# Two plain input-projection tiles of group A instead of four, and an eleventh pair computed with seven products

## The chip, the cores and the metric

The kernel runs on one core of one Trainium2 chip, as one program and one launch. The metric is the device time of an execution in microseconds (us), lower is better. An execution consists of the span, from the first to the last instruction of the program, and about 2 us around it.

## The reference

One step of a one-layer streaming encoder with two groups of attention heads, in float32. 640 tokens are processed together: 512 of a prompt and 8 x 16 of samples that extend cached sequences.

```python
def rmsnorm(x, g):
    return x * rsqrt(mean(x * x, -1) + 1e-6) * g

def layer(x):                                   # d_model 2048, x: 640 tokens
    p = rmsnorm(x, norm_mix) @ w_in             # columns: q, k, v of A (1024 each), q of B (1024), k, v of B (128 each)
    ...
    oa = band_attend(qa, ka, va, bias)          # 16 heads of 64: own chunk of 64 frames and 8 before, learned bias
    ob = band_attend(rope(qb), rope(kb), vb, sink)   # 16 query heads, 2 kv heads, window 128, sinks
    x = x + concat(rmsnorm(oa, g_a), rmsnorm(ob, g_b)) @ w_out
    h = rmsnorm(x, norm_ffn)
    x = x + (silu(h @ w_gate) * (h @ w_up)) @ w_down     # d_ff 5632
    return rmsnorm(x, norm_final)
```

Sample tokens attend to cached keys and values (256 of group A, 128 of group B) and to their own 16 frames. The new keys and values of both groups are returned too.

## The kernel before

Activations lie transposed, features on the 128 partitions and the 640 tokens along the free dimension, in two halves of 320. Every dense matmul is made of three (`mm3`, lines 207 to 209): both operands are split into a high and a low part (`split`: ScalarE makes the high part at L198, VectorE the low part at L199), and high x high, high x low and low x high are added up in PSUM. Each of these matmuls is 128 x 128 x 320.

The input projection gives 24 tiles of 128 features for group A, named (i, p): i is 0 for queries, 1 for keys, 2 for values, and p runs from 0 to 7. A tile is computed in one of two ways.

- **Plain** (`proj`, `dense`): 16 steps over the 2048 features, 2 token halves, 3 matmuls: 96 matmuls in a PSUM tile `dn`. Its evacuation is L382 or L384. After the six matmuls of a step `dense` calls `tick`, which lets side steps be written (`pump`), on average `n.rate` for each tick.
- **A pair by seven products** (`quartet`, `collect`): two output tiles, two token halves and two halves of the features form a 2 x 2 block product, which Strassen's scheme in Winograd's form makes with seven block products instead of eight: 7 x 8 x 3 = 168 matmuls for two tiles. The products read sums of activation blocks (`sums`). The first product's evacuation is L768, on ScalarE.

Sums of activation blocks are side work: `combine(k0, k1)` loads two tiles of x for each of its steps (L825, L826), scales one on ScalarE (L831), forms sums on VectorE (L832, L839) and GpSimd (L833, L835) and splits them. A third sum for each step is split later, in the first pair (`split_thirds`). Its x tiles use the two-tile slots of list W.

The other side work in this part is the rest of group B's attention: `prompt_b` for the prompt (queue "heads") and `decode_b` for the samples (queue "decode"). `decode_b` goes through eight batches, 0 to 7, with loads of cached keys (L552) and values (L553) ahead of batches 0 and 4. A batch is a chain of steps: scores of two kv heads on TensorE (L567, which the text calls the score), row maximum and sign on VectorE (L572, L573), exponents on ScalarE (L577, L578), normalization on VectorE (L579 to L582), four transposes on TensorE (L313), a copy on ScalarE (L592), the product with the values on TensorE (L597, called the weighing) and a copy on VectorE (L600). At its end `decode_b` stores its output (L603) and queues the last `combine(6, 8)`.

`pump` takes the streams in turn and writes one step of one of them. `drain` writes steps until none is left, `drain_queue` until one queue is empty, and `get` calls `pump` too while no slot of the wanted list is free. What is written is then ordered, engine by engine, by a scheduler that keeps dependences and puts ready work of other parts in between; `keep_pace` adds that a side matmul never stands before a plain or pair matmul that was written ahead of it. Engines and queues work through their instructions in the order so fixed.

After group B's eight query tiles the program reaches the loop at line 866: four plain tiles of group A, (1, 7), (0, 7), (2, 6) and (2, 7), at a rate of 1.15, with `drain_queue("heads")` after the second and `drain()` after the fourth. Ten pairs follow in the order of the list `order` (line 881); beside the last pair the heads of group A begin. Then come the output projection, the gate, up and down projections, and the final norm.

Of the kernel before, what the change touches and what calls it, by code (L numbers as in the profile page):

```python
# [291 lines left out]
def build(nc, tc, io, pools):  # L292
    n = Net(nc, tc, io, pools)
# [21 lines left out]
    def cut(hl, a, b):  # L315
        return hl[0][:, a:b], hl[1][:, a:b]
# [60 lines left out]
    def proj(idx, lst, ps=None, gain=None):  # L377
        if ps is None:
            ps = n.dense([(io["w_in"][idx, :, k:k + 8], 8) for k in (0, 8)], acts)
        out = n.get(lst)  # L380
        if gain is None:
            nc.vector.tensor_tensor(halves(out[:, :TOK]), ps, halves(r_mix), ALU.mult)  # L382
        else:
            nc.vector.scalar_tensor_tensor(halves(out[:, :TOK]), ps, gain, halves(r_mix), ALU.mult, ALU.mult)  # L384
        return out
# [424 lines left out]
    def keep_a(i, p, x):  # L810
        if i:
            dma(out=io["o_ka" if i == 1 else "o_va"][p], in_=x)
        dma(out=qkv_d[i, p], in_=x)
        n.put("S", x)
# [4 lines left out]
    def combine(k0, k1):  # L819

        tt, st = nc.gpsimd.tensor_tensor, nc.vector.scalar_tensor_tensor
        third = n.get("S" if k0 == 6 else "W")
        for kt in range(k0, k1):
            a, c = n.get("W"), n.get("W")
            dma(out=a[:, :TOK], in_=io["xT"][:, kt])  # L825
            dma(out=c[:, :TOK], in_=io["xT"][:, kt + 8])  # L826
            yield
            g = g_mix[:, kt + 8:kt + 9]
            a11, a21, a12, a22 = a[:, :HT], a[:, HT:TOK], c[:, :HT], c[:, HT:TOK]
            s1, s2 = a[:, TOK:TOK + HT], c[:, TOK:TOK + HT]  # L830
            nc.scalar.activation(a[:, :TOK], a[:, :TOK], AF.Identity, scale=g_mix[:, kt:kt + 1])  # L831
            st(s1, a22, g, a21, ALU.mult, ALU.add)  # L832
            tt(s2, s1, a11, ALU.subtract)  # L833
            s3 = third[:, HT * (kt % 3):HT * (kt % 3) + HT]
            tt(s3, a21, a11, ALU.subtract)  # L835
            thirds.append((third, s3))
            for which, x in ((3, s1), (1, s2), (6, a12)):
                if which == 6:
                    st(a12, a12, g, s2, ALU.mult, ALU.subtract)  # L839
                t = n.get("S")  # L840
                sums[kt][which] = t, pack(t, HT)
                n.split(x, *sums[kt][which][1])
            n.put("W", a, c)
            yield
# [17 lines left out]
    n.streams = (("heads 0", "heads"), ("decode 0", "decode"), ("combine", "combine"))  # L862
    n.add("combine", combine(0, 3))
    n.add("decode", decode_b())
    n.rate = 1.15
    for i, p in ((1, 7), (0, 7), (2, 6), (2, 7)):
        keep_a(i, p, proj(8 * i + p, "S", None, None if i else 0.125))
        if (i, p) == (0, 7):
            n.drain_queue("heads")
            n.move("Q", "S", 4)  # L870
            n.add("combine", combine(3, 6))
# [6 lines left out]
    for kt in range(8):  # L878
        for which, k, part in ((0, kt, 0), (2, kt, 1), (4, kt + 8, 0), (5, kt + 8, 1)):
            sums[kt][which] = None, cut(acts[k], HT * part, HT * part + HT)  # L880
    order = [(i, p + z) for p in range(0, 6, 2) for i in (1, 0, 2) for z in range(2)] + [(1, 6), (0, 6)]

    def group_operands(o_d, gain, ssq, tiles):
        own, out = [], []
# [509 lines left out]
```

## Time and profile before

| what | value |
|---|---|
| median of 3 runs | 2552.12 us (2551.49 to 2553.27) |
| profiled execution | 2550.54 us, span 2548.8 us |
| granted TensorE clock, mean | 0.993 |
| evacuation of plain tile (1, 7) | 212.0 us after the span's start |
| evacuation of plain tile (2, 7) | 282.4 us |
| first evacuations of pairs 1 and 10 | 286.75 and 516.13 us |

Times in the views are microseconds from the start of the span, unless a column says ns. PE is TensorE, PEld its weight loads, DVE VectorE, ACT ScalarE, POOL GpSimd, SP SyncE, which issues most of the DMAs. A row of the timeline gives start, duration, engine, line, operation, output<-inputs, shape and count, and in brackets the idle time before it and what ended that. Matmuls are pipelined: one takes 0.31 us from start to end, but they start 0.147 us apart in a full stream.

### The profile page before, as it was taken

The numbers are of one execution on the slowest core, as the hardware profiler recorded it, in microseconds if no ns is written. First come the engines' busy times: TensorE is split into PE (matmuls) and PEld (weight loads), VectorE is DVE, ScalarE is ACT, GpSimd is POOL, SyncE is SP. The second block draws the span as 40 slices with busy tenths as digits, with TensorE's granted clock in tenths as the row PEclk, the third lists the DMA queues.
The fourth block names the chain that finished last, engine by engine and source line by source line (L and its number), as shares of the span: only waits on it lengthen the run. The fifth ranks groups of instructions, "written<-read, shape, count | busy, mean of one in ns | idle before, by whom it ended". The sixth has DMA issues, their size and how long they took to land.

```text
span 2548.8 us, 44678 instructions
## 1 busy us (share of the span) xinstructions
PE 2496.6 (98%) x17325; PEld 2423.7 (95%) x17325; DVE 1949.0 (76%) x2928; ACT 1058.2 (42%) x1701; POOL 706.6 (28%) x568
## 2 busy tenths in 40 slices
PE   8999999999999999999999999999999999999997
PEld 8888899988789999999999999999999999999997
DVE  6666767685577787788888888888889877777797
ACT  5445333365455544344343334434334333333343
POOL 1001111120021123333232332323335433333353
PEclk9999999999999999999999999999999999999998
DMA  6234433376864434443334334434437756666655
GB/s 196 86 95 132 145 121 128 135 244 214 281 206 145 136 135 141 142 161 131 129 128 149 120 123 146 133 127 133 141 120 254 245 166 176 175 172 177 179 155 181
DMA packets 191605, 401.68 MB, mean 158 GB/s; under 512 B 22497, under 2 KB 83937, under 8 KB 191393
## 3 DMA queue, kind: packets, MB, share of 16 engines
q1 hardware_dynamic: 167056, 344.75, 41.5%
q0 software_dynamic: 23184, 52.77, 7.3%
q8 instruction: 136, 2.23, 0.4%
q10 hardware_dynamic: 1152, 1.31, 0.2%
q14 instruction: 77, 0.62, 0.1%
HBM read 311.14 MB, written 86.87 MB: 156 GB/s over the span
## 4 chain that ended last, share of the span: by engine, by line
PE 66%; DVE 4%; DMA 2%; issue 1%; ACT 1%; SPq 0%; DVEq 0%; ACTq 0%
PE dn L207 13%; PE dn L209 13%; PE dn L208 13%; PE at L209 9%; PE at L208 9%; PE at L207 9%; DVE W L199 2%; DVE S L759 1%; DMA W<-w_down 1%; PE at L313 0%; DVE S L1277 0%; DVE S L1085 0%; ACT S L410 0%; DVE W L737 0%; DMA x_d<-S 0%
## 5 line engine op out<-in xcount | busy, mean ns | idle before, releaser
L198 ACT ACTIVATE W<-W 128x1024 fp32r<-128x1024 f32 (+2 forms) x662 | 640.5, 968 | 1053.0 <-PE dn L208 558.8
L207 PE MATMUL dn<-S,W 128*128 128x320 f32 x3374 | 1058.3, 314 | 8.7 <-ACT W L198 5.7
L209 PE MATMUL dn<-S,W 128*128 128x320 f32 x3374 | 1047.2, 310 | 7.9 <-DVE W L199 7.9
L208 PE MATMUL dn<-S,W 128*128 128x320 f32 x3374 | 1045.4, 310 | 0.3 <-DVE S L199 0.3
L199 DVE TENSOR_TENSOR W<-W,W 128x1024 fp32r<-128x1024 f32 (+2 forms) x662 | 777.5, 1175 | 77.9 <-ACT W L198 74.3
L207 PEld LDWEIGHTS dn<-S,W 128*128 128x128 f32 x3374 | 635.5, 188 | 29.2 <-issue 17.2
L209 PEld LDWEIGHTS dn<-S,W 128*128 128x128 f32 x3374 | 634.9, 188 | 14.3 <-DVE W L199 11.8
L208 PEld LDWEIGHTS dn<-S,W 128*128 128x128 f32 x3374 | 635.6, 188 | 1.4 <-issue 0.9
L209 PE MATMUL at<-S,W 128*128 128x320 f32 x1834 | 568.8, 310 | 5.1 <-DVE W L199 5.0
L207 PE MATMUL at<-S,W 128*128 128x320 f32 x1834 | 568.3, 310 | 0.7 <-ACT W L198 0.7
L208 PE MATMUL at<-S,W 128*128 128x320 f32 x1834 | 567.8, 310 | 0.0
L740 POOL TENSOR_TENSOR W<-W,W 128x1024 f32<-128x1024 f32 (+2 forms) x85 | 183.2, 2156 | 754.7 <-DVE W L199 609.8
L209 PEld LDWEIGHTS at<-S,W 128*128 128x128 f32 x1834 | 345.3, 188 | 7.5 <-DVE W L199 7.5
L207 PEld LDWEIGHTS at<-S,W 128*128 128x128 f32 x1834 | 345.4, 188 | 1.1 <-ACT W L198 1.1
L208 PEld LDWEIGHTS at<-S,W 128*128 128x128 f32 x1834 | 345.5, 188 | 0.0
L759 DVE TENSOR_TENSOR S<-S,dn 128x320 f32<-128x320 f32 x398 | 182.2, 480 | 91.0 <-PE dn L209 90.4
L749 POOL TENSOR_TENSOR W<-W,W 128x1024 f32<-128x1024 f32 (+2 forms) x85 | 188.2, 2214 | 197.4 <-DVE W L199 145.4
L759 DVE TENSOR_TENSOR S<-S,at 128x320 f32<-128x320 f32 x292 | 137.7, 480 | 79.6 <-PE at L209 78.8
L735 DVE TENSOR_TENSOR W<-W,W 128x1024 f32<-128x1024 f32 (+2 forms) x86 | 135.0, 1570 | 70.0 <-DMA W<-w_down 35.8
L737 DVE TENSOR_TENSOR W<-W,W 128x1024 f32<-128x1024 f32 (+2 forms) x86 | 97.6, 1135 | 54.9 <-DMA W<-w_up 28.8
L1048 POOL DMA_DIRECT2D S<-act_d x161 | 88.0, 547 | 177.6 <-PE dn L209 92.1
L1112 DVE TENSOR_TENSOR S<-S,half 128x320 fp32r<-128x320 f32 x147 | 119.9, 836 | 1.9
(157 smaller groups left out, 1693.4 us busy)
## 6 DMA issues: line engine op xcount, KB each, us to landing
S<-act_d POOLq DMA_DIRECT2D x161, 320.0 KB, 3.8
W<-w_gate SPq DMA_DIRECT2D x88, 512.0 KB
W<-w_up SPq DMA_DIRECT2D x88, 512.0 KB
W<-w_in SPq DMA_DIRECT2D x66, 512.0 KB
W<-w_down SPq DMA_DIRECT2D x64, 384.0 KB
act_d<-half SPq DMA_DIRECT2D x147, 160.0 KB
act_d<-S SPq DMA_DIRECT2D x147, 160.0 KB
W<-w_down SPq DMA_DIRECT2D x68, 320.0 KB
```

Source lines behind the costliest of these rows:

```text
L198: self.nc.scalar.activation(hi, src, AF.Identity)
L199: self.nc.vector.tensor_tensor(lo, src, f(hi), ALU.subtract)
L207: mm(out, a[0], b[0], start=first, stop=False)
L208: mm(out, a[0], b[1], start=False, stop=False)
L209: mm(out, a[1], b[0], start=False, stop=last)
L735: nc.vector.tensor_tensor(b12[:, w], b12[:, w], b22[:, w], sub)
L737: nc.vector.tensor_tensor(s6[:, w], b11[:, w], b12[:, w], sub)
L740: eng.tensor_tensor(b11[:, w], b22[:, w], s6[:, w], sub)
L749: eng.tensor_tensor(b21[:, w], b21[:, w], s6[:, w], sub)
L759: add = lambda o, a, b: nc.vector.tensor_tensor(o, a, b, ALU.add)
L1048: nc.gpsimd.dma_start(out=r(sh(t, 2, HT)), in_=r(act_d[which, :, j]))
L1112: nc.vector.tensor_tensor(r(src), src, hi, ALU.subtract)
```

## The change

The loop of plain tiles keeps (1, 7) and (0, 7) alone, and the rate of side steps beside them is doubled from 1.15 to 2.3. `drain_queue("heads")`, the four slots and `combine(3, 6)` follow the first of the two tiles instead of the second of four. Tiles (2, 6) and (2, 7) become an eleventh pair at the end of the list, so that they are also the pair beside which group A's heads begin.

```diff
-    n.rate = 1.15
-    for i, p in ((1, 7), (0, 7), (2, 6), (2, 7)):
+    n.rate = 2.3
+    for i, p in ((1, 7), (0, 7)):
         keep_a(i, p, proj(8 * i + p, "S", None, None if i else 0.125))
-        if (i, p) == (0, 7):
+        if i:
             n.drain_queue("heads")
             n.move("Q", "S", 4)
             n.add("combine", combine(3, 6))
     n.drain()
...
-    order = [(i, p + z) for p in range(0, 6, 2) for i in (1, 0, 2) for z in range(2)] + [(1, 6), (0, 6)]
+    order = [(i, p + z) for p in range(0, 6, 2) for i in (1, 0, 2) for z in range(2)] + [(1, 6), (0, 6), (2, 6), (2, 7)]
```

How instructions move is seen in the order of each engine. First TensorE, around batch 5 of decode. Before, the weighing of batch 4 and the score of batch 5 are followed by the end of plain tile (2, 6), `dn_2667`, and the beginning of (2, 7), `dn_2930`:

```order
L597 MATMUL at_2878<-S_492_2870,S_470_2767 64x128 x2
L597 MATMUL at_2878<-S_492_2870,S_5_83 64x128 x2
L567 MATMUL at_2890<-S_469_2766,S_471_2768 128x144
L567 MATMUL at_2892<-S_469_2766,S_471_2768 128x144
L209 MATMUL dn_2667<-S_70_215,W_477_2786 128x320
L207 MATMUL dn_2667<-S_70_215,W_476_2785 128x320
L208 MATMUL dn_2667<-S_71_216,W_476_2785 128x320
L209 MATMUL dn_2667<-S_70_215,W_477_2786 128x320
L207 MATMUL dn_2930<-S_10_93,W_507_2932 128x320
```

Now, from the weighing of batch 3 on, TensorE's order is this:

```order
L597 MATMUL at_2610<-S_454_2598,S_346_2138 64x128 x2
L597 MATMUL at_2610<-S_454_2598,S_5_83 64x128 x2
L567 MATMUL at_2675<-S_461_2636,S_463_2638 128x144
L567 MATMUL at_2677<-S_461_2636,S_463_2638 128x144
L313 MATMUL at_2711<-cst,S_475_2684 128x128 x2
L313 MATMUL at_2711<-cst,S_479_2697 128x128 x2
L597 MATMUL at_2718<-S_481_2716,S_462_2637 64x128 x2
L597 MATMUL at_2718<-S_481_2716,S_5_83 64x128 x2
L567 MATMUL at_2730<-S_461_2636,S_463_2638 128x144
L567 MATMUL at_2732<-S_461_2636,S_463_2638 128x144
L313 MATMUL at_2772<-cst,S_488_2739 128x128 x2
L313 MATMUL at_2772<-cst,S_492_2752 128x128 x2
```

The matmuls of plain tiles no longer stand between the steps of batches 3 to 7: up to the weighing of batch 2 both orders have 192 of them, and behind it the new order has none before the transposes of batch 7, where the first pair begins.

Second ScalarE, at batch 3. `at_2634` and `at_2636` are the scores of its two kv heads before, L198 splits, L831 scales an x tile of `combine`, L592 is the copy after the transposes:

```order
L577 ACTIVATE S_445_2643,sm_2639<-at_2634,sm_2638 128x144
L578 ACTIVATE sm_2640<-sm_2638,gains 128x1
L198 ACTIVATE S_466_2750<-W_463_2730 128x320
L198 ACTIVATE S_467_2753<-W_464_2731 128x320
L577 ACTIVATE S_449_2656,sm_2652<-at_2636,sm_2651 128x144
L578 ACTIVATE sm_2653<-sm_2651,gains 128x1
L198 ACTIVATE S_468_2757<-W_464_2731 128x320
L592 ACTIVATE S_462_2722<-at_2717 128x512
L831 ACTIVATE W_473_2780<-W_473_2780,gains 128x640
```

Now, from the second kv head of batch 3 (`at_2523`) to the first of batch 4 (`at_2675`):

```order
L831 ACTIVATE W_465_2644<-W_465_2644,gains 128x640
L577 ACTIVATE S_441_2543,sm_2539<-at_2523,sm_2538 128x144
L578 ACTIVATE sm_2540<-sm_2538,gains 128x1
L198 ACTIVATE S_34_143<-W_447_2568 128x320
L592 ACTIVATE S_454_2598<-at_2593 128x512
L198 ACTIVATE S_467_2659<-W_465_2644 128x320
L198 ACTIVATE S_468_2662<-W_466_2645 128x320
L831 ACTIVATE W_526_2897<-W_526_2897,gains 128x640
L198 ACTIVATE S_469_2666<-W_466_2645 128x320
L577 ACTIVATE S_475_2684,sm_2680<-at_2675,sm_2679 128x144
```

The scaling of x tile 5 now stands ahead of batch 3's second exponent, and that of x tile 6 ahead of batch 4's first.

Third the queue of SP, where the loads of x (L825, L826), the cached keys and values of the second four batches (L552, L553), weights of pairs (L722) and the stores of tile (1, 7) (L812, L813) stand. Before:

```order
L812 DMA o_ka<-S_393_2382 128x640
L813 DMA qkv_d<-S_393_2382 128x640
L825 DMA W_463_2730<-xT 128x640
L213 DMA W_475_2784<-w_in 128x1024
L213 DMA W_506_2931<-w_in 128x1024
L826 DMA W_464_2731<-xT 128x640
L813 DMA qkv_d<-S_450_2664 128x640
L552 DMA S_469_2766<-ckb 128x4x128
```

Now:

```order
L722 DMA W_566_3204<-w_in 128x1024
L812 DMA o_ka<-S_442_2551 128x640
L813 DMA qkv_d<-S_442_2551 128x640
L826 DMA W_456_2607<-xT 128x640
L553 DMA S_462_2637<-cvb 128x512
L825 DMA W_465_2644<-xT 128x640
L519 DMA ob_d<-S_431_2510 128x512
L552 DMA S_461_2636<-ckb 128x4x128
L826 DMA W_466_2645<-xT 128x640
L825 DMA W_526_2897<-xT 128x640
```

The weights of the removed tiles (L213) are gone, a weight tile of the second pair stands ahead, and the keys of the second four batches stand between loads of x.

## The prediction

> **What bounds the kernel now.** I read the page first, then windows of busy time by stage, then the timeline of single operations. The page:
>
> ```profile
> span 2548.8 us, 44678 instructions
> PE 2496.6 (98%) x17325; PEld 2423.7 (95%) x17325; DVE 1949.0 (76%) x2928; ACT 1058.2 (42%) x1701; POOL 706.6 (28%) x568
> ...
> PE 66%; DVE 4%; DMA 2%; issue 1%; ACT 1%; SPq 0%; DVEq 0%; ACTq 0%
> ```
>
> TensorE is busy for 98% of the span and makes two thirds of the chain that ended last, so a product fewer should be time gained, but only where TensorE really is the bound. That is read from the stages (us of the stretch, busy time of each engine with its instructions, granted clock, DMA share, GB/s):
>
> ```profile
> core 0: us, PE busy (x) PEld busy (x) DVE busy (x) ACT busy (x) POOL busy (x), PEclk, DMA share, GB/s
> 212.00:236.50 24.50, 23.66 (x166) 20.05 (x165) 16.78 (x73) 15.39 (x49) 3.50 (x7) 1.00 0.26 88
> 236.50:281.68 45.18, 41.69 (x295) 35.91 (x294) 32.22 (x98) 23.50 (x62) 6.98 (x15) 0.96 0.47 154
> 281.68:317.30 35.62, 32.24 (x200) 30.42 (x198) 27.01 (x28) 11.19 (x14) 8.96 (x4) 0.95 0.46 154
> 392.32:490.93 98.61, 98.30 (x671) 98.00 (x670) 67.50 (x72) 31.01 (x34) 19.25 (x8) 1.00 0.37 130
> ```
>
> The last row is four steady pairs of seven products: 4 x 168 = 672 matmuls in 98.61 us, 146.7 ns each, no idle time. There TensorE is the bound. The second row is the stretch in which the plain tiles (2, 6) and (2, 7) stand now, with the decode of group B beside them: their 192 matmuls take 192 x 0.1467 = 28.2 us of its 45.2, and the other 17 us are side matmuls, waits and a lower clock. So what matters is what fills this stretch once the 192 are gone.
>
> **The products.** Two plain tiles go (192 matmuls, 28.2 us), one pair comes (168). Its price is read from the first evacuations of successive pairs on ScalarE:
>
> ```profile
> 286.75 0.42 ACT L768 ACTIVATE S<-dn 128x320 f32<-128x320 f32 x1
> 317.30 0.42 ACT L768 ACTIVATE S<-dn 128x320 f32<-128x320 f32 x1
> ...
> 392.32 0.42 ACT L768 ACTIVATE S<-dn 128x320 f32<-128x320 f32 x1
> ...
> 490.93 0.42 ACT L768 ACTIVATE S<-dn 128x320 f32<-128x320 f32 x1
> ```
>
> Four steady pairs: 98.61 / 4 = **24.65 us** for one more. The first pair takes 317.30 - 286.75 = 30.55, 5.9 over that. On a TensorE that is always full the change would be worth 24 x 0.1467 = 3.5 us of gain. The two removed weight tiles and evacuations (ScalarE and VectorE) lie beside matmuls, and the eleventh pair's preparation lies beside its own, as the steady pairs show; I cost both at nothing.
>
> **The side work.** 2.3 x 32 ticks are as many calls as 1.15 x 64, 73.6, so the same side work is written; what changes is what stands beside it on TensorE. Up to the weighing (L597) of decode batch 2 both programs have 192 plain matmuls and the same batches. From there to the first pair the old order has 192 more, spread through batches 3 to 7; the new one has none until the last batch's transposes are through. TensorE takes its instructions in that order, so the stretch becomes as long as the chain of five batches: score (L567), row maximum and exponent, transposes (L313), copy (L592), weighing (L597), next score. Scores and weighings of the old run:
>
> ```profile
> 231.70 0.39 PE L567 MATMUL at<-S,S 64*128 64x144 f32 x2
> 236.52 0.44 PE L597 MATMUL at<-S,S 128*64 128x128 f32 x4
> 238.62 0.39 PE L567 MATMUL at<-S,S 64*128 64x144 f32 x2
> 265.51 0.39 PE L567 MATMUL at<-S,S 64*128 64x144 f32 x2
> 274.09 1.12 PE L597 MATMUL at<-S,S 128*64 128x128 f32 x8
> 275.14 0.82 PE L567 MATMUL at<-S,S 64*128 64x144 f32 x4
> 281.09 0.66 PE L597 MATMUL at<-S,S 128*64 128x128 f32 x8
> ```
>
> They are batch 2 (score, weighing), batch 3 (score), batch 6 (score, weighing), batch 7 (score, weighing). Batch 2 needed 4.82 us from score to weighing, batch 7 5.95, batch 6 8.58. With the weighing itself (0.66) a batch takes from 5.5 to 9.6 us (265.51 to 275.14). What makes a slow one:
>
> ```profile
> 266.06 0.31 DVE L572 TENSOR_REDUCE sm<-at 128x1 f32<-128x144 f32 x1
> 266.79 1.22 DVE L735 TENSOR_TENSOR W<-W,W 128x1024 f32<-128x1024 f32 x1 [0.42 <-DMA W<-w_in]
> 267.93 0.21 DVE L573 TENSOR_SCALAR sm<-sm,gains 128x1 f32<-128x1 f32 x1
> ...
> 270.30 1.68 POOL L835 TENSOR_TENSOR S<-W 128x320 f32<-128x320 f32 x2 [5.80 <-PE at L313]
> 270.38 0.87 DVE L581 TENSOR_SCALAR S<-S,sm 128x128 f32<-128x128 f32 x1
> ```
>
> ```profile
> L581 DVE TENSOR_SCALAR S<-S,sm x16: 273/286/868, 216.2 to 279.0; 128x128 f32<-128x128 f32 x16
> ```
>
> In batch 6 VectorE's maximum was done at 266.37, but the next step (0.21 us) stood behind a preparation that waited for a load, and ran 1.6 us later; L581 took 0.87 us beside GpSimd's L835, where its median is 0.29 (least, median and greatest time in ns in the last row).
>
> Batches 3 and 4 of the new order carry most of this. Ahead of their exponents on ScalarE stands the scaling (L831) of the next x tiles, and ahead of their maxima on VectorE the sums (L832, L839) of `combine`, each behind a load into a slot that the tile before has just left. Such a load takes:
>
> ```profile
> 285.79 0.33 SPq L826 DMA_DIRECT2D W<-xT  x1
> 288.89 0.55 DVE L832 SCALAR_TENSOR_TENSOR W<-W,gains,W 128x320 f32<-128x320 f32 x1 [0.79 <-DMA W<-xT]
> ```
>
> 3.1 us from issue to use; on SP's queue they stand behind the store of tile (1, 7) and the next half's keys and values. Bounds for batches 3 and 4: 5.5 each (nothing late) to 9.6 each (as batch 6). I take 8.0 each, nearer to batch 6, since its kind of wait is there twice. Batches 5 and 6 have little ahead of them and are priced by batch 7: 5.95 + 0.66 = 6.6 each; batch 7 itself 5.95 to its weighing.
>
> Sum, from the weighing of batch 2 at 236.52: 2.1 to the score of batch 3 (238.62), 16.0, 13.2, 5.95: 37.3 us.
>
> **The clock.** TensorE has little to do in those 37 us. What that did before:
>
> ```profile
> 268.99:272.40 3.41, 1.96 (x13) 1.27 (x12) 3.06 (x10) 1.50 (x5) 1.68 (x2) 1.00 0.45 154
> 272.41:275.81 3.40, 3.40 (x19) 2.58 (x18) 1.28 (x3) 1.46 (x4) 0.00 (x0) 0.50 0.18 63
> ```
>
> After 3.4 us with 1.96 of matmuls the next 3.4 us had half the clock, and in them a weighing took 1.12 us, not 0.66. A batch alone has some 2 us of matmuls in 6, less than that, so I charge 0.46 for each of four weighings on the chain: 1.8 us. The Trainium skill ("TensorE: Matmul & The Clock Gate", Part 1) says of this that the slow clock is the default and that pauses beyond some 3.4 us bring it back, until a full window of activity has passed; it speaks against this change. By that rule the first pair would also begin with at least 3.4 us at half clock, 1.7 us more in the sum. The trace above agrees with the drop and its length. I leave that start out, since the first pair waits for something else, below.
>
> **Ahead of the gap.** Without two tiles to spread it over, VectorE gets one x tile more (two sums of 0.55), five thirds (L199) and one L735 (1.22) before batch 2 is weighed:
>
> ```profile
> 268.06 0.48 DVE L199 TENSOR_TENSOR S<-W,S 128x320 fp32r<-128x320 f32 x1
> ```
>
> 2 x 0.55 + 5 x 0.48 + 1.22 = 4.7 us. It is idle for 24.5 - 16.8 = 7.7 us of 212.0 to 236.5, so the cost lies between 0 and 4.7; I take 1.5, since most of it fits.
>
> **The first pair.** It overran by 5.9 us. Part is a wait that follows from the end of decode: the last x tile of `combine` uses the slot of the decode output, so its load (285.79, above) follows the store after the last weighing; that moves with the chain and stays. The rest of it, a clock drop and late weight tiles, may go, since those tiles now load during the gap: 0 to 5.9 of gain, I take 1.0.
>
> **Sum.** The weighing of batch 7 falls at 236.5 + 37.3 + 1.8 + 1.5 = 277.1 instead of 281.09: 4.0 earlier. In the old run the first pair starts at 281.68, right behind it, and in the new one just ahead of it. So -4.0 + 24.65 - 1.0 = **+19.6 us**. The profiled execution took 2550.54 us (2548.8 of span and 1.7 around it); that gives 2570.1, and the median of the runs shown, 2552.12, lies 1.6 higher: **2571 us**, slower by 0.75%.
>
> Low end: all five batches as batch 2: 2.1 + 4 x 5.5 + 4.8 = 28.9, weighing at 265.4, 15.7 earlier, +9.0; if the whole overrun of the first pair went as well, +3.1. High end: all as batch 6: 2.1 + 4 x 9.63 + 8.6 = 49.2, with 4.7 ahead 290.4, +34.
>
> **Rivals.**
> - Faster: the pair's matmuls cover the chain after all and TensorE stays full: -3.5, 2548.6 us, or 2543 if the 3.5 us of idle time and the clock loss of 236.5 to 281.7 go too. It decides where the last batch is weighed before 281.09 - 24.65 = 256.4, five batches in 20 us after batch 2. For it speaks only TensorE's 98%; against it the order, and that the fastest batch seen makes this 28.9 us. Chance 0.04.
> - The same: the fastest chain and a first pair without its overrun, +3.1, 2555 us. Against it: batches 3 and 4 have loads ahead of them, and the pair's last load hangs on the chain's end. Chance 0.05.
> - Much slower: the loads of `combine` and of the second half's keys block one another on SP's queue, and every batch runs as batch 6 did: +29 to +34, 2581 to 2586 us. For it speaks that in the new order each x tile waits for the slot of one just used; against it that batches 5 to 7 have almost nothing ahead. Chance 0.13.
> - My forecast, 0.78.
>
> **Numbers.** A change of less than 0.2% (5.1 us) can't be told from none. The range for 8 in 10 goes from the fastest chain, +9, to a little under the blocked one, +29: 2560 to 2582. Slower 0.91 (the forecast and the blocked chain), same 0.05, faster 0.04.
>
> **What would show it.** In the changed profile: from about 238 to 277 us TensorE busy for a third or less, with the clock at 0.50 for most of it; scores 5.5 to 7 us apart in the last batches, 7.5 to 9 around batches 3 and 4; the first L768 at about 282; nine further pairs 24.7 us apart and after them the old stages moved by about 20 us. Wrong would I be if plain matmuls stood between the batches, if scores followed each other in 4 us, or if later stages, which wait for other things, swallowed the shift.

## The result and the profile after

The changed kernel takes 2571.45 us (median of 4 runs, 2568.27 to 2574.06), the kernel before 2552.69 us on the same chip (4 runs, 2551.49 to 2554.32): a ratio of 1.0066 [1.0054, 1.0077]. The change makes the kernel 0.66% slower, 18.8 us between the medians; 2571 us was forecast. The profiled execution took 2572.52 us. The head of its page and its chain of work that ended last:

```profile
span 2570.7 us, 44659 instructions
PE 2499.2 (97%) x17301; PEld 2423.1 (94%) x17301; DVE 1968.6 (77%) x2940; ACT 1060.6 (41%) x1705; POOL 712.8 (28%) x570
...
PE 65%; DVE 4%; DMA 2%; issue 1%; ACT 1%; POOL 0%; DVEq 0%; ACTq 0%; POOLq 0%
```

The matmul records are 24 fewer than before, as the change says (168 for 192), and TensorE's busy time is no shorter: 2499.2 for 2496.6 us. Shares of the whole span tell next to nothing of a change in one stretch of 40 us. The windows do (us, busy time with instructions of PE, PEld, DVE, ACT and POOL, granted clock, DMA share, GB/s):

```profile
core 0: us, PE busy (x) PEld busy (x) DVE busy (x) ACT busy (x) POOL busy (x), PEclk, DMA share, GB/s
212.00:236.70 24.70, 23.45 (x166) 20.03 (x164) 18.73 (x78) 15.99 (x53) 4.23 (x7) 1.00 0.28 88
236.70:276.35 39.65, 18.05 (x98) 10.56 (x98) 24.42 (x87) 18.88 (x55) 7.27 (x15) 0.57 0.32 97
276.35:311.09 34.74, 32.01 (x203) 30.33 (x203) 26.93 (x28) 11.18 (x14) 8.59 (x4) 0.95 0.45 151
386.64:487.54 100.90, 99.69 (x673) 98.71 (x674) 69.18 (x72) 31.00 (x33) 19.34 (x8) 1.00 0.36 127
```

The second row is the gap: from the weighing of batch 2 to that of batch 7, 39.65 us in which TensorE has 98 matmuls and a granted clock of 0.57 in the mean. Its scores (L567) and weighings (L597), batch 2's weighing first, batch 7's last; what stands in brackets is TensorE's idle time before it and what ended that:

```profile
236.70 0.66 PE L597 MATMUL at<-S,S 128*64 128x128 f32 x8 [0.54 <-ACT S L592]
238.80 0.52 PE L567 MATMUL at<-S,S 64*128 64x144 f32 x4
246.22 1.12 PE L597 MATMUL at<-S,S 128*64 128x128 f32 x8 [0.73 <-ACT S L592]
247.28 0.85 PE L567 MATMUL at<-S,S 64*128 64x144 f32 x4
255.04 1.12 PE L597 MATMUL at<-S,S 128*64 128x128 f32 x8 [0.69 <-ACT S L592]
256.09 0.85 PE L567 MATMUL at<-S,S 64*128 64x144 f32 x4
261.37 1.12 PE L597 MATMUL at<-S,S 128*64 128x128 f32 x8 [0.69 <-ACT S L592]
262.42 0.85 PE L567 MATMUL at<-S,S 64*128 64x144 f32 x4
269.00 1.12 PE L597 MATMUL at<-S,S 128*64 128x128 f32 x8 [1.30 <-ACT S L592]
270.05 0.85 PE L567 MATMUL at<-S,S 64*128 64x144 f32 x4
276.35 1.12 PE L597 MATMUL at<-S,S 128*64 128x128 f32 x8
```

Scores follow each other at 8.48, 8.81, 6.33 and 7.63 us; the weighing of batch 7 comes 6.30 after its score. TensorE's waits between 236 and 282 us (line, what it waited for, us in total, times, longest):

```profile
PE at L313 <- DVE S L582: 13.5, 6, 3.8
PE at L313 <- DVE S L581: 4.1, 5, 2.2
PE at L597 <- ACT S L592: 4.0, 5, 1.3
PE dn L207 <- ACT W L198: 0.6, 1, 0.6
```

The transposes wait for VectorE's normalised weights, the weighings for ScalarE's copy: the decode chain. The last row is the first pair: its first matmul waited only 0.6 us for its split weights (L198), so the pair's weights come at nearly the same moment as the end of the chain.

In batches 3 and 4 the sums of `combine` do stand in the chain's way. In batch 4 ScalarE was done with the second kv head's exponents at 251.06, but VectorE's next step for them (L579) ran only at 252.45, behind a sum that waited for a load of x:

```profile
251.99 0.55 DVE L832 SCALAR_TENSOR_TENSOR W<-W,gains,W 128x320 f32<-128x320 f32 x1 [1.16 <-DMA W<-xT]
252.45 0.15 DVE L579 TENSOR_TENSOR sm<-sm,sm 128x1 f32<-128x1 f32 x1
```

In batch 3 the second maximum came behind a sum (L839) and the second exponent behind the scaling L831. Evacuations of pairs 1, 2, 10 and 11:

```profile
282.98 0.42 ACT L768 ACTIVATE S<-dn 128x320 f32<-128x320 f32 x1
311.09 0.42 ACT L768 ACTIVATE S<-dn 128x320 f32<-128x320 f32 x1
...
513.27 0.42 ACT L768 ACTIVATE S<-dn 128x320 f32<-128x320 f32 x1
538.68 0.42 ACT L768 ACTIVATE S<-dn 128x320 f32<-128x320 f32 x1
```

Before, the second pair stood at 317.30 (its row is above) and the tenth and last here:

```profile
516.13 0.42 ACT L768 ACTIVATE S<-dn 128x320 f32<-128x320 f32 x1
```

So the account of the profiled runs reads, against before:

| place | before | after | shift |
|---|---|---|---|
| weighing of batch 2 | 236.52 | 236.70 | +0.2 |
| weighing of batch 7 | 281.09 | 276.35 | -4.7 |
| evacuation, pair 1 | 286.75 | 282.98 | -3.8 |
| evacuation, pair 2 | 317.30 | 311.09 | -6.2 |
| evacuation, pair 10 | 516.13 | 513.27 | -2.9 |
| evacuation, last pair | 516.13 | 538.68 | +22.6 |
| end of span | 2548.8 | 2570.7 | +21.9 |

Taking 28.2 us of matmuls out of the stretch brought the second pair forward by 6.2 us; 3.4 of these are lost over the next eight pairs, and the eleventh pair costs its 25.4 us at the far end. The stages behind keep the shift to within 0.7 us.

### The profile page after: what moved, and what is told of

Same layout as the page of the kernel before. It is cut to its first block, busy times and chain, and to the rows that moved or that the text cites. A ratio compares the mean times of both kernels' runs of the same rounds, so it can differ in the third digit from the quotient of the medians.

```text
span 2570.7 us, 44659 instructions
## 1 busy us (share of the span) xinstructions
PE 2499.2 (97%) x17301; PEld 2423.1 (94%) x17301; DVE 1968.6 (77%) x2940; ACT 1060.6 (41%) x1705; POOL 712.8 (28%) x570
## 4 chain that ended last, share of the span: by engine, by line
PE 65%; DVE 4%; DMA 2%; issue 1%; ACT 1%; POOL 0%; DVEq 0%; ACTq 0%; POOLq 0%
PE dn L207 13%; PE dn L209 13%; PE dn L208 13%; PE at L209 8%; PE at L207 8%; PE at L208 8%; DVE W L199 2%; DMA W<-w_down 1%; DVE S L759 1%; PE at L313 0%; PE at L436 0%; DMA W<-w_gate 0%; DVE S L1277 0%; DVE W L737 0%; ACT S L410 0%
## 5 line engine op out<-in xcount | busy, mean ns | idle before, releaser
L198 ACT ACTIVATE W<-W 128x1024 fp32r<-128x1024 f32 (+2 forms) x665 | 643.4, 968 | 1071.4 <-PE dn L208 581.1
L199 DVE TENSOR_TENSOR W<-W,W 128x1024 fp32r<-128x1024 f32 (+2 forms) x665 | 781.8, 1176 | 81.1 <-ACT W L198 77.8
L209 PE MATMUL at<-S,W 128*128 128x320 f32 x1858 | 575.2, 310 | 4.2 <-DVE W L199 4.2
L207 PE MATMUL at<-S,W 128*128 128x320 f32 x1858 | 574.5, 309 | 0.7 <-ACT W L198 0.6
L208 PE MATMUL at<-S,W 128*128 128x320 f32 x1858 | 574.1, 309 | 0.0
L735 DVE TENSOR_TENSOR W<-W,W 128x1024 f32<-128x1024 f32 (+2 forms) x87 | 139.8, 1607 | 73.2 <-DMA W<-w_down 33.4
```

What stands on the lines that cost most here:

```text
L198: self.nc.scalar.activation(hi, src, AF.Identity)
L199: self.nc.vector.tensor_tensor(lo, src, f(hi), ALU.subtract)
L207: mm(out, a[0], b[0], start=first, stop=False)
L208: mm(out, a[0], b[1], start=False, stop=False)
L209: mm(out, a[1], b[0], start=False, stop=last)
L735: nc.vector.tensor_tensor(b12[:, w], b12[:, w], b22[:, w], sub)
```

## The experiments

Theory (the cover theory): the stretch is as long as the chain of decode batches when nothing stands beside it, and the plain tiles were free there. Rivals: TensorE is the bound everywhere, so that each matmul costs its own time; the doubled rate crowds VectorE and ScalarE ahead of the gap; the loads of `combine` and of the first pair make the gap; the half clock makes it. All but the changed kernel ran on two other chips, on which the kernel before took 2554 to 2556 us, so each is told by its ratio to that kernel on its own chip; the ratio to set it against is the change's 1.0066 [1.0054, 1.0077], and 0.0010 of it is 2.6 us.

**The tiles without the rate, and the rate without the tiles.** The changed kernel at the old rate:

```diff
-    n.rate = 2.3
+    n.rate = 1.15
```

> Two plain tiles and eleven pairs as in the change, but the rate of side steps left at 1.15. Theory (cover): the loss is the stretch in which decode batches 3 to 7 stand alone on TensorE, whatever the rate, because what the ticks do not write the drains write and the scheduler places it the same way: 2571, within 5 us of the change. Rival (crowding): the doubled rate crowds VectorE and ScalarE beside the two tiles, and without it most of the loss is gone: 2560 or less.

Measured: 2574.81 us, ratio 1.0072 [1.0057, 1.0088]: the change's. The first pair's evacuations stand at 283.08 and 311.18 (282.98 and 311.09). The higher rate does nothing here: at either rate the weighings of batches 3 to 7 come behind the two tiles (the last at 276.22, 276.35 in the change). The other half, on the kernel before:

```diff
-    n.rate = 1.15
+    n.rate = 1.7
```

> Four plain tiles and ten pairs as before, with the rate raised to 1.7 (side work is done before the fourth tile ends). Theory (cover): the batches keep their plain matmuls, so nothing is lost; the last x tile of combine is loaded before the fourth tile ends, so the first pair may lose part of its 5.9 us of overrun: 2545 to 2554. Rival (crowding): a rate raised by half costs a good part of what the change cost: 2560 or more.

Measured: 2561.9 us, ratio 1.0022 [1.0013, 1.0032]. Slower, as the crowding theory had it, but not by its mechanism. Decode ended sooner (its output's store was issued at 273.16), no batch stood bare, and a wait that neither theory named took the place. TensorE's longest wait from 260 to 300 us, and then SP's queue:

```profile
PE dn L207 <- ACT W L198: 12.1, 2, 11.6
```

```profile
273.16 0.38 SPq L603 DMA_DIRECT2D ob_d<-W  x1
274.36 0.34 SPq L812 DMA_DIRECT2D o_va<-S  x1
274.75 1.37 SPq L813 DMA_DIRECT2D qkv_d<-S  x1
279.62 0.33 SPq L826 DMA_DIRECT2D W<-xT  x1
280.06 0.37 SPq L722 DMA_DIRECT2D W<-w_in  x1
```

The first pair's weight load (L722) stands in the queue behind an x load (L826) that was issued only at 279.62, 3.5 us after the entry ahead of it had ended; it waited for the store of the decode output (L603), whose slot it takes. A later weight load then waited 4.0 us until splits on VectorE (L199) left it a slot, and the pair's first product waited 11.6 us for its split weights. So the pair stage has a floor of its own, set by these loads and the slots that they wait for; a shorter decode stage alone runs into it.

**Half of the decode work.** Batches 4 to 7 are left out, and their half of the output is filled with zeros, in the changed kernel and in the one before:

```diff
-        for hf in range(2):
+        nc.gpsimd.memset(os_b, 0.0)
+        for hf in range(1):
```

> The changed kernel without decode batches 4 to 7 of group B (their output is left at zero). Theory (cover): four batches at 6.3 to 8.8 us each leave the gap, 29 us, but then the sums of combine end last and the first pair waits for them, so 18 to 28 us less than the change: 2544 to 2553. Rival (TensorE is the bound everywhere): only the batches' own matmuls go, 4 x 2 us: 2563.

> The old kernel without decode batches 4 to 7 (their output is left at zero). Theory (cover): beside plain matmuls four batches cost about their own matmuls and the waits of the drain, 8 to 14 us less than the old kernel, where the same cut took 17 us from the change. Rival (the batches cost the same wherever they stand): 17 us less or more.

Measured: 2556.55 us, ratio 1.0007 [0.9998, 1.0017] with two plain tiles, 15 us under the change by the ratios: short of the 18 to 28 of the cover theory, and nearly twice the 8 of its rival. With four: 2533.55 us, ratio 0.9922 [0.9905, 0.9938], 20 us under the kernel before, where at most 14 was expected of the cover theory; 17 or more was the rival's, that the batches cost the same wherever they stand. So the cover theory missed both totals, and the profiles have to tell what each is made of. With two tiles TensorE has this (the last weighing, then the first pair):

```profile
246.19 1.12 PE L598 MATMUL at<-S,S 128*64 128x128 f32 x8 [0.74 <-ACT S L593]
265.99 0.63 PE L207 MATMUL dn<-S,W 128*128 128x320 f32 x1 [18.68 <-ACT W L198]
```

Decode is over at 247.3, and the pair still starts only at 265.99, 9.5 us ahead of the 275.52 of the changed kernel. This is the floor of the loads again: the weight loads on SP's queue stand behind those of x and waited 9.2 us in all for slots that VectorE's splits (L199) leave. With four tiles the first pair's evacuation comes at 278.98 (286.75 before, -7.8, about what the matmuls of four batches take) and the second at 305.25 (-12.1): most of the first pair's overrun, part of which waits for the end of decode, went as well. In the profiled runs 9.4 us are left at the last pair and 14.8 at the end; later stages scatter (from the last pair's evacuation to the end the fourteen profiled kernels of this study took between 2027.2 and 2037.6 us), and what is lacking to 20 no profile shows. With two tiles the second pair gains 13.0 us (298.05 for 311.09). That is nearly the same, so this pair of runs does not tell cover from its rival; the next one does.

**Plain matmuls put back.** The changed kernel with eleven pairs, and tile (2, 6), or (2, 6) and (2, 7), computed as plain tiles as well, their results thrown away. The rate is 1.15, and what follows the first tile in the change follows the second, as before:

```diff
-    for i, p in ((1, 7), (0, 7)):
+    for i, p in ((1, 7), (0, 7), (2, 6)):          # or also (2, 7)
...
+        if i == 2:
+            n.put("S", x)
```

> Three plain tiles at rate 1.15, the third's result, tile (2, 6), thrown away, and eleven pairs: 96 matmuls (14.1 us of TensorE) more than the change. Theory (cover): they stand beside batches 3 to 5 in time that these take anyhow, and bring the clock back: 0 to 4 us over the change, 19 to 23 over the old kernel. Rival (each matmul costs its 0.147 us): 14 over the change, 33 over the old kernel.

> Eleven pairs as in the change, and all four plain tiles at rate 1.15 as before; the plain results of tiles (2, 6) and (2, 7) are thrown away, so this is 192 matmuls (28.2 us of TensorE) more than the change. Theory (cover): the 192 matmuls stand in time that the batches take anyhow, so this is the old kernel plus one pair, 2552 + 24.65 = 2577, some 5 us over the change. Rival (TensorE is the bound everywhere): 2571 + 28 = 2599.

Measured: one spare tile 2573.87 us, ratio 1.0081 [1.0066, 1.0096]; two 2581.3 us, ratio 1.0097 [1.0079, 1.0115]. Here is the cover itself. The same stretch, 236.5 to 282.0 us, with none, one and two spare tiles:

```profile
236.50:282.00 45.50, 23.68 (x129) 15.79 (x130) 29.02 (x90) 20.13 (x56) 9.64 (x16) 0.59 0.34 103
```

```profile
236.50:282.00 45.50, 32.64 (x200) 25.07 (x197) 32.45 (x98) 22.39 (x60) 7.60 (x16) 0.75 0.34 115
```

```profile
236.50:282.00 45.50, 41.28 (x292) 35.97 (x293) 32.01 (x98) 23.66 (x63) 7.02 (x15) 0.96 0.44 138
```

Each spare tile adds 96 matmuls, 14.1 us at full pitch. Against the change one costs 0.0015 of the ratio, which the intervals do not tell from none, and both 0.0031, 8 us, with intervals apart; against the changed kernel at the old rate, which ran on the same chip, both cost 0.0025, 6 us. In the profiles the second pair comes 3.2 us later with one (314.24) and 6.0 with both (317.13). So the two plain tiles cost the kernel before 6 to 8 us for 28.2 us of matmuls, and spared it a pair of 24.65: this is the sign of the change. The pair's price can be read here too: with both spare tiles the kernel is the one before and a pair more, and takes 0.0097, 24.8 us, longer.

**The decode output in small slots.** Its output goes into a slot of the small pool per half of the batches, each stored when done, so that no x load of `combine` waits for the large slot:

```diff
-        os_b = n.get("W")
         for hf in range(2):
+            os_b = n.get("S")
...
-            n.put("S", ko, vo, qo)
+            n.put("S", ko, vo, qo, os_b)
```

> The changed kernel with the output of decode batches kept in a slot of list S for each half, so that list W has one slot more for the x tiles of combine and the last of them need not wait for the store of decode. Theory: decode's own chain sets the end of the gap, so batches 3 to 7 still stand alone; only the waits for loads go, about 1 to 2 us in each of batches 3 and 4 and 3 us of the first pair's overrun: 4 to 9 us less than the change, so 10 to 15 us over the old kernel. Rival (the loads of combine on SP's queue are what makes the gap, the decode only goes along): the gap falls to under 25 us and the time to within 5 us of the old kernel.

> The old kernel (four plain tiles, ten pairs, rate 1.15) with the same move of the decode output. Theory: its batches are covered by plain matmuls, so only the first pair's wait for the last x tile and its clock drop can go: 3 to 6 us less than the old kernel. Rival (that wait was only the visible end of others, as late weight tiles): within 2 us of the old kernel.

Measured: 2573.08 us, ratio 1.0074 [1.0057, 1.0092], and on the kernel before 2552.98 us, ratio 0.9995 [0.9984, 1.0006]. No gain in either. The theory missed both times; its rival for the kernel before (within 2 us) came, its rival for the changed one (a gap under 25 us) did not. In the changed kernel the gap is 38.7 us (39.65) and begins 3.2 us later (batch 2 is weighed at 239.94): batches 3 and 4 get shorter (6.74 and 7.66 us from score to score) and batch 5 longer (8.04). In the kernel before the first pair's overrun is gone, 24.45 us for 30.55, and the second pair comes 4.6 us sooner (312.68), of which 1.8 are left at the end of the profiled run. The loads behind that store do not make the gap alone; that several waits end close together would fit, but is not shown.

**The clock in the gap.** 18 matmuls that nobody reads, behind the score of each of batches 3 to 7; the decode chain itself keeps its steps:

```diff
+    def spare(ps, k):
+        for i in range(k):
+            nc.tensor.matmul(ps[:, :HT], acts[15][0][:, :P], acts[15][0][:, :HT], start=i == 0, stop=i == k - 1)
...
+                ps = n.bank()
+                spare(ps, 18 * (b > 2))
```

> The changed kernel with 18 matmuls (128x128 by 128x320) whose result nobody reads behind the score of each of the batches 3 to 7, ahead of the same batch's transposes and in the bank that these then overwrite: 90 more matmuls, which are 13 us at 0.147 us each, all of them where TensorE stands bare. It separates the granted clock from the chain of engines that sets the gap. If the gap is a chain that is longer because TensorE runs at half clock in it: the granted clock no longer falls to 0.50 there, the gap of 39.65 us becomes about 36 us, and the kernel takes 2 to 5 us less than the changed one although it does more. If the clock plays no part, since TensorE waits for VectorE either way: within 1 us of the changed kernel. If each spare matmul costs its own time: 13 us more.

Measured: 2572.18 us, ratio 1.0059 [1.0045, 1.0073]. The gap, from the weighing of batch 2 to that of batch 7:

```profile
236.75:272.22 35.47, 27.05 (x188) 21.97 (x188) 23.30 (x87) 18.93 (x55) 7.28 (x15) 0.95 0.36 108
```

With 90 more matmuls the clock stays at 0.95 in the mean, and the gap is 4.2 us shorter, not longer: the half clock stretches the whole chain, not its weighings alone. The first pair's weights come sooner too: its first product starts at 271.74 for 275.52, so in this kernel they went along with the chain. The first pair's evacuation comes at 278.99 and the second pair's at 306.41, 4.0 and 4.7 us ahead of the change. In the kernel's time, where 2 to 5 us were expected, this is 0.0007 of the ratio, 1.8 us, which these intervals do not tell from none; in the profiled run the later stages took 3.6 us more than the change's. So the clock's part in the gap is shown, its part in the time is not.

**Two decode streams.** The two halves of the batches become two streams that the planner places side by side, in the changed kernel:

```diff
-    def decode_b():
+    def decode_b(half):
...
-    n.add("decode", decode_b())
+    n.add("decode", decode_b(0))
+    n.add("decode", decode_b(1))
```

> The changed kernel with the decode work as two streams, one for each half of four batches, that the planner places side by side instead of one behind the other; all else is left. It separates the decode chain from the loads that follow it. If the gap is the one chain of score, maximum, transposes and weighing, two chains side by side fill each other's waits: the first pair starts near 266 us (where it started with the decode work halved, held there by the loads of its tiles and weights) instead of 275.5, and the kernel takes 8 to 16 us less than the changed one. If the loads behind the decode output set the gap, the start of the first pair moves little: at most 5 us less.

Measured: 2565.51 us, ratio 1.0031 [1.0019, 1.0044], 9 us under the change, with intervals apart. The chain got much shorter; TensorE, the last weighing and then the first pair:

```profile
256.35 1.12 PE L602 MATMUL at<-S,S 128*64 128x128 f32 x8 [0.69 <-ACT S L597]
273.32 0.63 PE L207 MATMUL dn<-S,W 128*128 128x320 f32 x1 [15.85 <-ACT W L198]
```

Decode is over at 257.5, not 277.5, and yet the first pair starts at 273.32 for 275.52. SP's queue shows what came ahead of its weights:

```profile
250.23 0.32 SPq L519 DMA_DIRECT2D ob_d<-S  x1
251.29 0.33 SPq L834 DMA_DIRECT2D W<-xT  x1
...
264.02 0.33 SPq L834 DMA_DIRECT2D W<-xT  x1
264.39 8.58 SPq L730 DMA_DIRECT2D W<-w_in  x4
```

The x loads of `combine` are let go after a store that waits until 250.23 for ScalarE's output of the heads, each into a slot that another has left, and the first pair's four weight loads follow from 264.39 on, with 6.9 us of waits for slots that VectorE's splits leave. Of the cover theory's expectation the start near 266 fell and the time, 8 to 16 us less, came, though by another way; that of the loads, a start that moves little, held, but its bound on the time, at most 5 us less, fell: the first pair then runs without its overrun (24.49 us for 28.11), and the second pair's evacuation is 4.1 us ahead of the change's. In the changed kernel the gap has two ends that fall together: the decode chain at 276.35 and the weights at 275.52. With a chain 4.1 us shorter (the spare matmuls) the weights came 3.8 sooner; with one 20 us shorter they came only 2.2 sooner. So the loads are a second bound, close behind the chain; whether their order on the queue or the slots that they wait for set it, no run here separates.

The same with the output in small slots, and the two streams on the kernel before:

> As the one with two streams and two plain tiles, and the output of each half goes into a slot of the small pool and is stored when its half is done, so that the combine stage's x loads don't stand behind one store at the end. If the decode chain alone sets the gap: the same 8 to 16 us less than the changed kernel, within 2 us of the other. If the decode output's slot and store hold the loads once the chain is short: 3 to 8 us less than the other.

> The kernel before (four plain tiles, ten pairs, rate 1.15) with the decode work as two streams and its outputs in slots of the small pool. If the last batches of the kernel before were bare only because the one chain is slow: all eight batches are covered by the plain tiles, the first product of the pair stage comes some 6 to 10 us sooner, and the kernel takes 2543 to 2550 us where the one before takes 2552 to 2555 us. If the first pair's weights and x loads, which stand on SP's queue in one order, cannot come sooner, a wait for weights of about 10 us takes the place of the bare batches, as in the kernel before at rate 1.7: 2553 us or more.

Measured: with two plain tiles 2570.22 us, ratio 1.0058 [1.0046, 1.0070]: the expectations of neither theory came. The store of the first half (issued at 256.49 after a wait of 17.9 us for decode) now stands ahead of the x loads on SP's queue, and the pair starts at 280.62, though decode is over at 262.5. With four plain tiles 2546.61 us, ratio 0.9957 [0.9945, 0.9969]: 0.43% faster than the kernel before, and so faster than both. Its stretch:

```profile
236.00:263.00 27.00, 26.68 (x192) 21.40 (x191) 15.54 (x66) 15.14 (x45) 4.30 (x11) 1.00 0.31 86
```

TensorE is full at clock 1.00, every batch stands beside plain matmuls, and the last weighing is at 258.58. The pair stage does not begin the 6 to 10 us sooner that were expected, but 1.8 (279.86 for 281.68), right behind the last plain tile; it then waits 2.3 us for split weights (L199), and its first evacuation comes at 287.09 for 286.75. But the first pair loses most of its overrun, and the second comes 4.0 us sooner (313.32). So the expected time, 2543 to 2550, came, by another way. The 0.43% is 11 us; the profile of one run shows 4.0 of them here, and 0.8 at the last pair. Where the rest lies is open, since its profiled run was the slowest of its five and the kernel before was not profiled on that chip.

## Why the prediction was right, point by point

- **The sign and the sum.** +19.6 us forecast; +21.9 in the profiled runs, +18.8 between the medians. What carried it, that the plain matmuls were cover and the pair is not, is shown by the spare tiles: 28.2 us of matmuls for 6 to 8. That the forecast came out within 0.5 us of the median is luck: single terms were off by 0.7 to 3.4 us in both directions (below), and the profiled and the median shifts themselves differ by 3.1. My own sum gives 2571.7, not 2571.
- **The chain, 37.3 us and 1.8 for the clock.** 39.1 forecast, 39.65 measured. Batch by batch, measured in brackets: 2.1 (2.10), 8 and 8 (8.48 and 8.81), 6.6 and 6.6 (6.33 and 7.63), 5.95 (6.30), where the measured values hold the clock's part. The reason given for the slow batches 3 and 4, sums and scalings of `combine` ahead of their steps, is in the trace (above). Batch 6 was not free of it: its copy (L592) stood behind two splits that waited for GpSimd's L835, and its weighing waited 1.30 us for it. The split of the sum was mis-sized: with the clock at 0.95 the chain took 35.47, so the clock is worth about 4.2 us, not 1.8, and the batches about 35.5, not 37.3; the two misses cancel. I charged the half clock on the weighings alone; scores (0.85 for 0.52) and transposes are on the chain too.
- **Ahead of the gap, +1.5.** Batch 2 is weighed at 236.70, 0.2 late: the low bound, 0, was nearly the value. With that the weighing of batch 7 fell 4.7 us sooner, not 4.0.
- **The clock at the pair's start.** I left the Trainium skill's rule ("TensorE: Matmul & The Clock Gate", Part 1: a full window of activity before the fast clock) out of the sum, on the ground that the pair would be waiting. It was not waiting. From the last weighing to the first evacuation, after and then before:

```profile
276.35:282.98 6.63, 6.61 (x38) 6.20 (x38) 4.61 (x4) 2.02 (x3) 2.37 (x1) 0.72 0.54 158
```

```profile
281.09:286.75 5.66, 5.66 (x43) 5.42 (x43) 4.72 (x5) 2.02 (x2) 2.42 (x1) 1.00 0.61 199
```

  TensorE is busy throughout at a clock of 0.72, and the same way takes 1.0 us more. The rule agrees with the trace, and the 1.7 us that I had estimated by it was nearer than my 0. The drop itself I had read too simply: in the stretch of the kernel before that I showed for it TensorE's longest pause was 0.57 us, not the 3.4 that I named.
- **The first pair, -1.0.** It takes 28.11 us for 30.55, so it gave 2.4 back, within the bounds of 0 and 5.9. That its last x load hangs on the end of decode is only part of what is left: with that store out of the way the first pair took 26.55 in the changed kernel.
- **The eleventh pair, +24.65.** It took 25.41. The eight intervals from the second pair to the tenth average 25.27 us, 24.85 before, 3.4 us in all that I had not foreseen. VectorE's L735 waited longer for w_in loads (8.5 us over all pairs, 3.2 before). The change is not needed for it: four kernels with four plain tiles and ten pairs (rate 1.7, output in small slots, half decode, two streams) had 25.14, 25.03, 25.19 and 25.26. The kernel before has the shortest pairs of all fourteen profiles. Why the loads take longer in one run than in another is open.
- **What would show it.** The clock was 0.50 from 242.5 to 280.0 us, and the first L768 came at 282.98 for 282, as forecast. TensorE was busy for 18.05 of the 39.65 us, 46%, where I had said a third or less: at half clock each record is longer (a weighing 1.12 us for 0.66). The scores of batches 6 and 7 stood 7.63 us apart, where I had said 7 at most for the last ones.
- **The rivals.** Faster fell with the order: nothing stood beside batches 3 to 7. Blocked loads: the batches did not run as batch 6 did, but the loads bound the stage nearly at the same moment as the chain, and a much shorter chain meets them. My forecast had no place for this: it asked only when the chain ends, but the gap's end is the later of two terms. The low end of my range, a chain of 28.9 us with the last weighing at 265.4, would have met them too: with decode over at 247.3 the pair started at 265.99, and with two streams, decode over at 257.5, at 273.32. The rival that gave no change needed that short chain, and the chain was 39.65 us.

## What to carry to other kernels

Before fewer instructions on a full engine are counted as time, ask what stands beside them: matmuls that cover a slow chain of small steps on other engines cost a fraction of their length (6 to 8 of 28 us here), and taking them away leaves the chain bare and the clock at half. Where a chain and a queue of loads end close together, shortening the chain gives only part of what it saves (its end 20 us sooner, the start of the next stage 2.2, the kernel 9): look on the queue that issues the loads for a store or an x load that waits ahead of them. Two chains side by side, with the cover kept, made the kernel 0.43% faster here; where most of that came from is open.

## What the runs showed of the hardware

Work that nobody reads can shorten a stretch: 90 more matmuls, 13 us of them at the full pitch, held the granted clock at 0.95 for 0.57 and made the gap 35.47 us for 39.65. The clock is granted in stretches of some 3.4 us: the half clock lasted 3.41 us from 272.40 and again from 296.30 in the kernel before, and 37.55, eleven times as long, from 242.47 in the changed one. What TensorE did in one stretch shows in the next. Five stretches of the changed kernel, one ahead of the half clock and four in it (columns as in the windows above):

```profile
239.05:242.47 3.42, 0.27 (x4) 0.05 (x2) 2.53 (x8) 2.49 (x8) 1.30 (x3) 1.00 0.80 232
242.47:245.88 3.41, 1.35 (x4) 0.69 (x4) 3.11 (x12) 1.86 (x6) 1.33 (x2) 0.50 0.80 217
...
259.50:262.90 3.40, 2.46 (x16) 1.55 (x14) 0.87 (x4) 0.60 (x1) 0.42 (x2) 0.50 0.00 0
...
273.20:276.60 3.40, 2.43 (x8) 1.45 (x10) 2.87 (x8) 2.41 (x6) 0.00 (x0) 0.50 0.01 2
276.60:280.00 3.40, 3.38 (x17) 2.98 (x16) 3.32 (x4) 0.80 (x1) 2.37 (x1) 0.50 0.37 104
```

One nearly idle stretch (0.27 us) brought the half clock at 242.47, and stretches that were busy for up to 2.46 us, with no wait behind 243.1 longer than 2.71 us, kept it there until 276.60; the full one (3.38) ended it at 280.0. With the spare matmuls a stretch of 3.29 us, in the half clock from 246.0 to 249.4, was enough to end it. But the busy time of a stretch alone draws no border. With two plain tiles, two streams and the output in small slots:

```profile
240.10:243.50 3.40, 3.11 (x15) 2.11 (x15) 2.06 (x13) 1.24 (x7) 0.20 (x1) 0.50 0.04 14
281.10:284.50 3.40, 2.97 (x11) 2.57 (x11) 3.21 (x4) 1.62 (x3) 3.11 (x2) 0.50 0.38 127
```

The first, busier one was followed by another at 0.50, the second by one at 1.00. The same holds for the drop: it came after 1.96 us busy in the kernel before, and not after 1.64 (1974.8 to 1978.2 us, the kernel before with its output in small slots). What else decides, no run shows.
